# Turning the last two chunk pairs of the first token half in 64-row pieces

## The chip, the cores and the metric

The kernel runs on one core of one Trainium2 chip. The metric is device time in microseconds (us) of one execution. The engines are named as in the profile: PE (TensorE), ACT (ScalarE), DVE (VectorE), POOL (GpSimd) and SP (the engine that issues most of the loads). Each runs its own list of instructions in order, and waits on semaphores for the others.

## What is computed

One layer of a diffusion backbone: modulated RMSNorm, a mixing sub-layer (pooling and neighbourhood attention), a residual, then a squared-ReLU MLP and another residual. The change is in the MLP, at the point where its input is made:

```python
x = x + gt1 * _rmsnorm(mix_x, g_post_mix[l])
y_x = _sq_relu_mlp(_modulate(x, g_pre_mlp[l], sh2, sc2), w_mlp_in[l], w_mlp_out[l])
x = x + gt2 * _rmsnorm(y_x, g_post_mlp[l])

def _modulate(x, gain, shift, scale):
    return _rmsnorm(x, gain) * (1 + scale) + shift
def _sq_relu_mlp(h, w1, w2):
    return jnp.square(jax.nn.relu(h @ w1)) @ w2
```

There are 1024 tokens, 1024 features and 4096 hidden columns, all in float32.

## The kernel before

**Products.** Every matrix product is made of float32r pieces: an operand is split into a high part (a cast on ACT, L169 or L171) and a low part (a subtraction on DVE, L175 or L177), and `three` (L221 to L223) adds high times high, high times low and low times high. The MLP's input product is done in 2 by 2 blocks by a scheme of Strassen's kind: features in halves, tokens in halves, hidden columns in halves. B11 is the first half of the features of the first 512 tokens, B21 the second half of the features of the same tokens.

**Making B11 and B21.** The first 512 tokens lie in four pages `mp1[0..3]` of 128 tokens by 1024 features, already divided by their root mean square. The products need features on the partitions, so PE turns each 128 by 128 block against the identity. A chunk is 128 features; two chunks make a pair `kp`, four pairs in all. For one pair, `transposed` (L1647) makes eight transposes into two banks of PSUM `px`, one bank for a chunk with 512 tokens. `normal_pair` (L1656) copies each bank out on ACT with one instruction of 128 by 512, which applies the modulation as scale and shift per partition (for pairs 2 and 3 with the sign turned) into a page `nf0_<kp>`. `token_part` then casts the page (1024 wide) to its high part `thB` on ACT (L169) and subtracts for its low part `tlB` on DVE (L175). Pairs 0 and 1 make B11, pairs 2 and 3 make B21.

**The order around it.** `last_product` writes this stage by hand: the last four output products of the mixing sub-layer (`pov`, PE) stand between the transposes of pairs 0 and 1, then come pairs 2 and 3 directly behind each other. Between them stand `more()` calls, each of which splits one piece of the MLP's weights `wpA` (ACT L169 or L171, then DVE L175 or L177), and `first_less(7)` (DVE L1524), which empties the last bank `pov`. Behind `last_product` follows the first group of MLP products, two hidden blocks at a time: block 0 times B11 into bank `phx0`, block 1 times B11 into `phx1`, then block 0 times B21 added into `phx0`, block 1 times B21 into `phx1`. Twelve matmuls of 128 by 512 make one of these products. Between the first and the second product of a block, ACT copies the bank's first sum away to `s` (`first_kept`, L1893), since the scheme needs it alone; so the B21 product of a block can only begin when that copy is done.

The order on ACT and DVE is fixed to that of the program by `in_order`, and PE's as well (`first_order`). Work that is `stepwise` puts the DVE half of a split behind the next weight piece (`caught_up`), but not yet in `last_product`.

**The other half.** The second 512 tokens are turned later (`second_half`) by functions that exist already: `side_pair` (L1750) turns 64 tokens by 128 features at a time, from rows 0 to 63 of each page into one bank and from rows 64 to 127 into another, alternating between the two. `normal_sides` (L1762 on DVE, L1764 on ACT) copies out by chunk and side: four instructions of 128 by 256 for a pair, which write runs of 64 tokens. For pairs 0 and 2 one side, two of the four, goes to DVE; the rest go to ACT.

Of the kernel before, what the change touches and what calls it, by code (L numbers as in the profile page):

```python
# [13 lines left out]
AF = mybir.ActivationFunctionType  # L14
# [4 lines left out]
P = 128  # L19
# [7 lines left out]
HD = 64  # L27
# [76 lines left out]
def hybrid_block(ctx, tc, x, ctx_in, w_mod, mod_pages, w_u, b_mod, gp1, gp2, w_in, pool_w, rpb, w_out, w1, w2, vectors,  # L104
                 mask, edge, out):
    nc = tc.nc
    sub, mul, add = ALU.subtract, ALU.mult, ALU.add
# [8 lines left out]
    def cst(name, shape, dt=F32):  # L116
        return const.tile(shape, dt, tag=name, name=name)

    def sm(name, n, bufs=1):
        return small.tile([P, n], F32, tag=name.split("_")[0], name=name, bufs=bufs)  # L120

    def page(name, dt=F32):
        return act.tile([P, 1024], dt, tag="pg", name=name)
# [21 lines left out]
    ident = cst("ident", [P, P])  # L145
# [45 lines left out]
    def step_split(src, hi, lo, factor=1.0):  # L191
        high_part(src, hi, factor)
        second = lambda: low_part(src, hi, lo, factor)
        if stepwise:
            behind.append(second)
        else:
            second()
# [90 lines left out]
    def lasting(name):  # L288
        return ps_t.tile([P, 512], F32, tag="T", name=name)

    sx = cst("sx", [P, KT])
    a2, s2 = cst("a2", [P, KT]), cst("s2", [P, KT])

    with tc.tile_pool(name="ps1", bufs=6, space=PSUM) as ps1, tc.tile_pool(name="tmp1", bufs=3) as tmp:

        def bank(name):
            if name[:2] == "pm" or name in ("pxt5", "pxb2", "pxb3", "pxb4", "pxb5", "pct2", "pct3"):
                return lasting(name)
            return ps1.tile([P, 512], F32, tag="mm", name=name)
# [76 lines left out]
        on_act, on_dve = nc.scalar.copy, nc.vector.tensor_copy  # L376
# [121 lines left out]
        whole, pt = {}, {}  # L498
# [242 lines left out]
        for k in range(KT):  # L741
            for i in range(2):
                o = (k % 2) * 256 + i * P
# [423 lines left out]
    with (  # L1167
# [4 lines left out]
        bank = lasting  # L1172
# [158 lines left out]
        mp1 = {}  # L1331


        def out_sums(ps, a, w, t, begin):
            for k in range(4):
                mp = mix[a][k]
                three(ps, mp[:, t * P : (t + 1) * P], mp[:, 512 + t * P : 512 + (t + 1) * P],
                      wk(w, k, 0, 0, 512), wk(w, k, 1, 0, 512), begin and k == 0, k == 3, more=not begin)
# [32 lines left out]
        with in_order(ET.PE, ET.Activation, ET.DVE, ET.SP) as projected:  # L1371
# [31 lines left out]
            for i in range(N + 4):  # L1403
# [43 lines left out]
                else:  # L1447

                    t = i - N
# [57 lines left out]
    with tc.tile_pool(name="ps2", bufs=6, space=PSUM) as ps2:  # L1507
# [6 lines left out]
      with ExitStack() as tmp2:  # L1514
# [117 lines left out]
        less_a2, less_s2 = sm("na2", 8), sm("ns2", 8)  # L1632
# [5 lines left out]
        plain = {}  # L1638


        def transposed(kp):
            pts = []
            for o in range(2):
                k = 2 * kp + o
                pt = bank(f"px0_{k}")
                for i in range(4):
                    nc.tensor.transpose(pt[:, i * P : (i + 1) * P], mp1[i][:, k * P : (k + 1) * P], ident)  # L1647
                pts.append(pt)
            return pts

        def normal_pair(kp, pts):
            f = page(f"nf0_{kp}")
            a, d = (a2, s2) if kp < 2 else (less_a2, less_s2)
            for o, pt in enumerate(pts):
                k = 2 * kp + o
                nc.scalar.activation(f[:, o * 512 : (o + 1) * 512], pt, AF.Identity, bias=d[:, k : k + 1],  # L1656
                                     scale=a[:, k : k + 1])
            return f

        def token_part(name, kp, f):  # L1660
            hi, lo = page(f"th{name}_{kp}", F32R), page(f"tl{name}_{kp}", F32R)
            step_split(f, hi, lo)
            tok[name, kp] = hi, lo

        def pair_made(kp, pts):
            plain[0, kp] = normal_pair(kp, pts)
            token_part("B11" if kp < 2 else "B21", kp % 2, plain[0, kp])


        def first_less(t):  # L1670
            c[t, 0] = out_less(0, t, v[t - 4], u2[t - 4])

        def gate_steps(h, t):
            src = c[t] if h else c[t, 0]
            out_square(h, t, src)
            out_gated(h, t, src)

        def last_product():
            for t in range(2):
                out_sums(v[t], "A22", wt4, t, False)  # L1680
            first_less(4)
            more()
            pts = transposed(0)
            first_less(5)
            pair_made(0, pts)
            more()
            out_sums(v[2], "A22", wt4, 2, False)
            pts = transposed(1)
            first_less(6)
            gate_steps(1, 6)  # L1690
            pair_made(1, pts)
            more()
            out_sums(v[3], "A22", wt4, 3, False)
            pts = transposed(2)
            first_less(7)
            pair_made(2, pts)
            pts = transposed(3)
            more()
            pair_made(3, pts)

# [38 lines left out]
            yield  # L1739


        def side_pair(kp):
            pts = [bank(f"px1_{2 * kp + h}") for h in range(2)]
            for o in range(2):
                ks = slice((2 * kp + o) * P, (2 * kp + o + 1) * P)
                for i in range(4):
                    at = (4 * o + i) * HD
                    for h in range(2):
                        hs = slice(h * HD, (h + 1) * HD)
                        nc.tensor.transpose(pts[h][:, at : at + HD], mp1[4 + i][hs, ks], ident[hs, hs])  # L1750
            return pts

        def normal_sides(kp, pts):
            f = page(f"nf1_{kp}")
            by_side = f.rearrange("p (o i h t) -> p o h i t", o=2, i=4, h=2)
            a, d = (less_a2, less_s2) if kp < 2 else (a2, s2)
            for h in range(2):
                for o in range(2):
                    k = 2 * kp + o
                    to, pt = by_side[:, o, h], pts[h][:, o * 256 : (o + 1) * 256].rearrange("p (i t) -> p i t", i=4)  # L1760
                    if kp % 2 == 0 and h == (kp == 2):
                        nc.vector.tensor_scalar(to, pt, a[:, k : k + 1], d[:, k : k + 1], mul, add)  # L1762
                    else:
                        nc.scalar.activation(to, pt, AF.Identity, bias=d[:, k : k + 1], scale=a[:, k : k + 1])  # L1764
            return f

        def second_half():
            nf = dict((kp, normal_sides(kp, side_pair(kp))) for kp in (0, 2, 1, 3))
            return [nf[0], nf[1]], [nf[2], nf[3]]

        def second_steps(b12, b22):
            b21 = [plain[0, 2 + kp] for kp in range(2)]
            t1, t2 = [[page(f"t{i}_{kp}") for kp in range(2)] for i in (1, 2)]
            source = {"T1": t1, "T2": t2, "T3": b12, "T4": b21, "B22": b22}

            def combined(kp):
                nc.vector.tensor_tensor(t1[kp], b12[kp], plain[0, kp], add)
                add_to(b12[kp], b22[kp])
                nc.vector.tensor_tensor(t2[kp], b22[kp], t1[kp], add)
                add_to(b21[kp], t2[kp])  # L1780

            for kp in range(2):
                combined(kp)
                yield
            for name in ("T2", "T1", "T3", "B22", "T4"):
                for kp in range(2):
                    token_part(name, kp, source[name][kp])
                    yield
# [90 lines left out]
        def more():  # L1879
            ready.extend(islice(coming_parts, 1))  # L1880
# [185 lines left out]
        with tc.issue_after(added[ET.DVE]), tc.issue_after(added[ET.Activation]), in_order(ET.Activation, ET.DVE) as first_part:  # L2066
            last_product()
            stepwise.append(True)
            between, xs, ending = row_steps(), {}, None
            for p in range(0, EARLY, 2):  # L2070
                for sum in (1, 2):
                    for q in (p, p + 1):
                        if ending:
                            ending()
                        caught_up()
                        if (q, sum) == (5, 2):
                            between = second_steps(*second_half())
                        if sum == 1:
                            xs[q] = bank(f"phx{q}")
                        step(xs[q], "B11" if sum == 1 else "B21", sum == 1)  # L2080
                        next(between, None)
                        if sum == 1:
                            ending = lambda q=q: early.update({q: first_kept(q, xs[q])})
                        else:
                            ending = lambda q=q: second_kept(q, xs[q])
            ending()
            caught_up()
            for _ in between:
                caught_up()
            caught_up()  # L2090
            stepwise.clear()
# [166 lines left out]
```

## Time and profile before

| | |
|---|---|
| median of three runs | 1022.59 us (1022.5 to 1023.45) |
| the profiled execution's own time | 1022.56 us |
| its span, first to last instruction | 1020.8 us |
| around the span | 1.76 us |
| PE busy | 1010.3 us |
| ACT, DVE busy | 547.1 us, 744.4 us |
| mean granted clock of PE | 0.999 |

A row of the timeline gives the start in us from the span's start, the length in us, the engine, the line, the operation with output and input by the program's names (buffer numbers left out), and how many instructions were merged (x2). In brackets stands idle time before it and what ended it. Instructions of one engine overlap at their ends, so the distance from start to start tells what one costs in a row of them, and the length tells when its result is there.

### The profile page before, as it was taken

The page shows a single profiled execution, that of the slowest core. Times are in us where ns is not written, and L with a number is a line of the kernel's source. Part 1 is how long each engine was busy: PE and PEld are TensorE (multiplying, and loading weights), DVE is VectorE, ACT ScalarE, POOL GpSimd, SP SyncE. Part 2 cuts the span into 40 slices and gives each one's busy share as a digit, 9 for nine tenths or more (in the row PEclk, how much of TensorE's full clock was granted, in tenths as well). Part 3 has the DMA queues.
Part 4 walks back from the last instruction along what each step waited for, and adds up shares of the span by engine and source line. Part 5 has one row for each costly group of instructions (what it writes and reads, how often), then busy time and mean ns, then how long its engine had stood idle before and what let it go on. Part 6 is the DMA issues. An engine that isn't in the chain of part 4 may idle for free.

```text
span 1020.8 us, 16178 instructions
## 1 busy us (share of the span) xinstructions
PE 1010.3 (99%) x5970; PEld 834.5 (82%) x5970; DVE 744.4 (73%) x1161; ACT 547.1 (54%) x958; POOL 155.1 (15%) x235
## 2 busy tenths in 40 slices
PE   8999999999999999999999999999999999999997
PEld 5788888878998888888888888888888888888886
DVE  5588767877885688879988888755757666557576
ACT  7682255348986747786555554555543343334431
POOL 4111210166774221410000000000000000000002
PEclk9999999999999999999999999999999999999999
DMA  9899798641448945886786667437967766555555
GB/s 365 317 275 324 252 267 295 206 102 44 95 95 203 233 183 196 280 213 201 256 261 206 214 197 228 174 134 250 347 217 260 253 222 216 198 183 189 170 181 224
DMA packets 117023, 222.72 MB, mean 218 GB/s; under 512 B 9488, under 2 KB 46992, under 8 KB 116944
## 3 DMA queue, kind: packets, MB, share of 16 engines
q1 hardware_dynamic: 90448, 171.14, 49.5%
q0 software_dynamic: 9360, 19.58, 9.4%
q10 hardware_dynamic: 17136, 30.97, 8.1%
q8 instruction: 47, 0.77, 0.3%
q14 instruction: 32, 0.26, 0.1%
HBM read 168.16 MB, written 52.45 MB: 216 GB/s over the span
## 4 chain that ended last, share of the span: by engine, by line
PE 96%; DMA 2%; DVE 0%; ACT 0%; issue 0%; SPq 0%; DVEq 0%; POOLq 0%; ACTq 0%
PE pu L469 4%; PE pa L1276 4%; PE S L1196 3%; PE phx L221 3%; PE phz L221 3%; PE phv L221 3%; PE pyx L221 3%; PE phx L222 3%; PE pyz L223 3%; PE phv L222 3%; PE pyv L223 3%; PE phz L222 3%; PE pyx L223 3%; PE phx L223 3%; PE pyv L221 3%; PE pyz L221 3%
## 5 line engine op out<-in xcount | busy, mean ns | idle before, releaser
L1222 ACT ACTIVATE sp<-sp,nm 128x640 f32<-128x640 f32 (+1 forms) x64 | 51.4, 803 | 10.9 <-DVE ri L1226 5.0
L1211 DVE CUSTOM_DVE_ANT_0 sp<-S,tab 128x640 f32<-128x640 f32 (+1 forms) x56 | 44.5, 795 | 14.0 <-PE pz L1242 10.6
L169 ACT CAST wpS<-S 128x512 fp32r<-128x512 f32 x64 | 38.8, 616 | 28.2 <-PE phv L223 10.1
L1842 ACT ACTIVATE c<-c 128x512 f32<-128x512 f32 x48 | 30.3, 631 | 43.6 <-DVE c L1962 24.9
L221 PE MATMUL phx<-thB,wpA 128*128 128x512 f32 x128 | 50.3, 393 | 0.0
L222 PE MATMUL phx<-tlB,wpA 128*128 128x512 f32 x128 | 49.9, 390 | 0.0
L223 PE MATMUL phx<-thB,wpA 128*128 128x512 f32 x128 | 49.9, 390 | 0.0
L175 DVE TENSOR_TENSOR wpS<-S,wpS 128x512 fp32r<-128x512 f32 x64 | 43.4, 686 | 8.2 <-ACT wpS L169 8.2
L163 POOL TENSOR_TENSOR ry<-vy,nhalf 128x1 f32<-128x1 f32 x8 | 5.9, 740 | 281.5 <-DVE vy L161 281.5
L1843 ACT ACTIVATE c<-c 128x512 f32<-128x512 f32 x48 | 30.3, 631 | 15.2 <-DVE sa L1925 10.5
L221 PEld LDWEIGHTS phx<-thB,wpA 128*128 128x128 f32 x128 | 24.0, 188 | 5.7 <-ACT s L1893 0.6
L223 PEld LDWEIGHTS phx<-thB,wpA 128*128 128x128 f32 x128 | 24.1, 188 | 5.0
L222 PEld LDWEIGHTS phx<-tlB,wpA 128*128 128x128 f32 x128 | 24.1, 188 | 4.8
L1276 PE MATMUL pa<-pt,v 128*64 128x128 f32 x352 | 25.9, 280 | 0.2
L1261 DVE COPY pt<-T 128x512 f32<-128x512 f32 x32 | 21.9, 686 | 5.5 <-PE T L1242 5.5
L221 PE MATMUL phz<-thB,wpS 128*128 128x512 f32 x64 | 25.1, 392 | 0.0
L221 PE MATMUL phv<-thT,wpA 128*128 128x512 f32 x64 | 25.0, 391 | 0.0
L223 PE MATMUL phz<-thB,wpS 128*128 128x512 f32 x64 | 25.0, 390 | 0.0
L222 PE MATMUL phz<-tlB,wpS 128*128 128x512 f32 x64 | 24.9, 390 | 0.0
L223 PE MATMUL phv<-thT,wpA 128*128 128x512 f32 x64 | 24.9, 390 | 0.0
L222 PE MATMUL phv<-tlT,wpA 128*128 128x512 f32 x64 | 24.9, 390 | 0.0
L223 PE MATMUL phy<-thT,wpS 128*128 128x512 f32 x64 | 24.9, 390 | 0.0
(1144 smaller groups left out, 3434.3 us busy)
## 6 DMA issues: line engine op xcount, KB each, us to landing
b<-in_w SPq DMA_DIRECT2D x64, 512.0 KB, 4.1
hrS<-hdS SPq DMA_DIRECT2D x32, 512.0 KB, 5.3
hrA<-hdA SPq DMA_DIRECT2D x24, 512.0 KB, 5.3
wm<-in_mod_pages SPq DMA_DIRECT2D x16, 512.0 KB, 9.6
wa_0w<-in_w SPq DMA_DIRECT2D x16, 512.0 KB, 4.8
wa_1w<-in_w SPq DMA_DIRECT2D x16, 512.0 KB, 4.3
hdA<-c ACTq DMA_DIRECT2D x32, 256.0 KB, 2.5
hdS<-sa ACTq DMA_DIRECT2D x32, 256.0 KB, 2.5
```

Of the source, the lines that this page charges most:

```text
L169: nc.scalar.copy(hi, src)
L175: nc.vector.tensor_tensor(lo, src, hi.bitcast(F32), sub)
L221: nc.tensor.matmul(ps, ahi, bhi, start=first, stop=False, skip_group_check=more)
L222: nc.tensor.matmul(ps, ahi, blo, start=False, stop=False, skip_group_check=more)
L223: nc.tensor.matmul(ps, alo, bhi, start=False, stop=last, skip_group_check=more)
L469: nc.tensor.matmul(pus[b][j], wk(wgt, k, low, j * P, P), r, start=(k == 0 and n == 0), stop=(k == KT - 1 and n == 2))
L1196: nc.tensor.matmul(S[e][:, c0 : c0 + k[0].shape[1]], q[n_q][hs, cols], k[n_k][hs], start=(n_q + n_k == 0), stop=(n_q == 1))
L1211: nc.vector.tensor_tensor_reduce(out=to, in0=s, in1=bt, scale=1.0, scalar=BIG, op0=add, op1=ALU.min, accum_out=nm)
L1222: nc.scalar.activation(sp, sp, AF.Exp, bias=least[i, e], scale=-1.0, accum_out=sums[i][:, e : e + 1])
L1276: nc.tensor.matmul(pa[e * HD : (e + 1) * HD, cols], v[:, f : f + HD], turns[i][:, e, c] if c < 4 else fifths[i][:, :, (e + 1) * HD : (e + ...
L1842: nc.scalar.activation(r, src, AF.Relu)
L1843: nc.scalar.activation(r, r, AF.Square)
```

## The change

`side_pair` and `normal_sides` move ahead of `last_product` and take the token half `b` as an argument, with the side that DVE copies passed in. The second half calls them as before. In the first half, pairs 2 and 3 now use them: pair 2 with all four copies on ACT, pair 3 with side 1 (two copies) on DVE and side 0 on ACT. Pairs 0 and 1 keep `transposed` and `normal_pair`.

```diff
+        def side_pair(b, kp):
+            pts = [bank(f"px{b}_{2 * kp + h}") for h in range(2)]
+            for o in range(2):
+                ks = slice((2 * kp + o) * P, (2 * kp + o + 1) * P)
+                for i in range(4):
+                    at = (4 * o + i) * HD
+                    for h in range(2):
+                        hs = slice(h * HD, (h + 1) * HD)
+                        nc.tensor.transpose(pts[h][:, at : at + HD], mp1[4 * b + i][hs, ks], ident[hs, hs])
+            return pts
+
+        def normal_sides(b, kp, pts, on_dve):
+            f = page(f"nf{b}_{kp}")
+            by_side = f.rearrange("p (o i h t) -> p o h i t", o=2, i=4, h=2)
+            a, d = (less_a2, less_s2) if (kp < 2) == (b == 1) else (a2, s2)
+            for h in range(2):
+                for o in range(2):
...
+                    if h == on_dve:
+                        nc.vector.tensor_scalar(to, pt, a[:, k : k + 1], d[:, k : k + 1], mul, add)
+                    else:
+                        nc.scalar.activation(to, pt, AF.Identity, bias=d[:, k : k + 1], scale=a[:, k : k + 1])
+            return f
+
         def pair_made(kp, pts):
-            plain[0, kp] = normal_pair(kp, pts)
+            plain[0, kp] = normal_pair(kp, pts) if kp < 2 else normal_sides(0, kp, pts, (None, 1)[kp - 2])
             token_part("B11" if kp < 2 else "B21", kp % 2, plain[0, kp])
...
-            pts = transposed(2)
+            pts = side_pair(0, 2)
             first_less(7)
             pair_made(2, pts)
-            pts = transposed(3)
+            pts = side_pair(0, 3)
             more()
             pair_made(3, pts)
...
         def second_half():
-            nf = dict((kp, normal_sides(kp, side_pair(kp))) for kp in (0, 2, 1, 3))
+            nf = dict((kp, normal_sides(1, kp, side_pair(1, kp), (0, None, 1, None)[kp])) for kp in (0, 2, 1, 3))
```

On PE, behind the last `pov` product, pair 2 stood before as eight transposes of whole blocks, one bank after the other (`px_4` and `px_5` are the banks, `mp_0` to `mp_3` the pages of tokens; a row's size is that of its output):

```order
L1647 MATMUL px_4_5239<-ident,mp_0_4632 128x128
L1647 MATMUL px_4_5239<-ident,mp_1_4642 128x128
L1647 MATMUL px_4_5239<-ident,mp_2_4652 128x128
L1647 MATMUL px_4_5239<-ident,mp_3_4656 128x128
L1647 MATMUL px_5_5244<-ident,mp_0_4632 128x128
L1647 MATMUL px_5_5244<-ident,mp_1_4642 128x128
L1647 MATMUL px_5_5244<-ident,mp_2_4652 128x128
L1647 MATMUL px_5_5244<-ident,mp_3_4656 128x128
```

Now it begins with these eight, and the same eight follow for the second chunk; pair 3 goes in the same way into `px_6` and `px_7`:

```order
L1668 MATMUL px_4_5239<-ident,mp_0_4632 128x64
L1668 MATMUL px_5_5240<-ident,mp_0_4632 128x64
L1668 MATMUL px_4_5239<-ident,mp_1_4642 128x64
L1668 MATMUL px_5_5240<-ident,mp_1_4642 128x64
L1668 MATMUL px_4_5239<-ident,mp_2_4652 128x64
L1668 MATMUL px_5_5240<-ident,mp_2_4652 128x64
L1668 MATMUL px_4_5239<-ident,mp_3_4656 128x64
L1668 MATMUL px_5_5240<-ident,mp_3_4656 128x64
```

So 16 transposes become 32, and both banks of a pair are finished only with the pair's last two transposes, where the first bank was finished after four of eight.

On ACT, from the weight piece ahead of pair 2 to the copy that frees `phx0` for its B21 product, stood before:

```order
L171 ACTIVATE wpA_0_5224<-wa0w 128x512
L1656 ACTIVATE nf_2_5251<-px_4_5239,ns_5067,na_5066 128x512
L1656 ACTIVATE nf_2_5251<-px_5_5244,ns_5067,na_5066 128x512
L169 CAST thB_0_5254<-nf_2_5251 128x1024
L171 ACTIVATE wpA_1_5268<-wa1w 128x512
L1656 ACTIVATE nf_3_5271<-px_6_5258,ns_5067,na_5066 128x512
L1656 ACTIVATE nf_3_5271<-px_7_5263,ns_5067,na_5066 128x512
L169 CAST thB_1_5274<-nf_3_5271 128x1024
L169 CAST wpA_2_5281<-wa2w 128x512
L1893 COPY s_0_5295<-phx_5278 128x512
```

and now stands:

```order
L171 ACTIVATE wpA_0_5224<-wa0w 128x512
L1682 ACTIVATE nf_2_5259<-px_4_5239,ns_5067,na_5066 128x4x64 x2
L1682 ACTIVATE nf_2_5259<-px_5_5240,ns_5067,na_5066 128x4x64 x2
L169 CAST thB_0_5264<-nf_2_5259 128x1024
L171 ACTIVATE wpA_1_5286<-wa1w 128x512
L1682 ACTIVATE nf_3_5289<-px_6_5268,ns_5067,na_5066 128x4x64 x2
L169 CAST thB_1_5294<-nf_3_5289 128x1024
L169 CAST wpA_2_5301<-wa2w 128x512
L1893 COPY s_0_5315<-phx_5298 128x512
```

Two copies of pair 2 became four, each half as wide; two copies of pair 3 became two, each half as wide. Nothing else on ACT moved. The cast `thB_1` reads the whole page `nf_3`, which DVE now writes in part.

On DVE, in the same stretch (`co_7` is `first_less(7)`), stood before:

```order
L1524 TENSOR_TENSOR co_7_5249<-pov_4913,so_1_4390 128x512
L175 TENSOR_TENSOR tlB_0_5255<-nf_2_5251,thB_0_5254 128x1024
L177 SCALAR_TENSOR_TENSOR wpA_1_5268<-wa1w,wpA_1_5268 128x512
L175 TENSOR_TENSOR tlB_1_5275<-nf_3_5271,thB_1_5274 128x1024
L175 TENSOR_TENSOR wpA_2_5281<-wa2w,wpA_2_5281 128x512
```

and now stands:

```order
L1524 TENSOR_TENSOR co_7_5257<-pov_4913,so_1_4390 128x512
L175 TENSOR_TENSOR tlB_0_5265<-nf_2_5259,thB_0_5264 128x1024
L177 SCALAR_TENSOR_TENSOR wpA_1_5286<-wa1w,wpA_1_5286 128x512
L1680 TENSOR_SCALAR nf_3_5289<-px_7_5269,na_5066,ns_5067 128x4x64 x2
L175 TENSOR_TENSOR tlB_1_5295<-nf_3_5289,thB_1_5294 128x1024
L175 TENSOR_TENSOR wpA_2_5301<-wa2w,wpA_2_5301 128x512
```

DVE's two copies of pair 3 stand behind the low part of pair 2 (`tlB_0`) and a weight piece (`wpA_1`). In the rest of the program the engines' rows are the same as before, in the same order.

More of the change, by code (lines that the diff above doesn't have):

```diff
@@ L1658, in normal_pair @@
             return f
+        def side_pair(b, kp):
[14 more added lines that the diff above has]
+                for o in range(2):
+                    k = 2 * kp + o
+                    to, pt = by_side[:, o, h], pts[h][:, o * 256 : (o + 1) * 256].rearrange("p (i t) -> p i t", i=4)
+                    if h == on_dve:
[3 more added lines that the diff above has]
+            return f
         def token_part(name, kp, f):
@@ L1739, in row_steps @@
             yield
[L1742 to L1765, printed above, removed]
         def second_half():
-            nf = dict((kp, normal_sides(kp, side_pair(kp))) for kp in (0, 2, 1, 3))
+            nf = dict((kp, normal_sides(1, kp, side_pair(1, kp), (0, None, 1, None)[kp])) for kp in (0, 2, 1, 3))
             return [nf[0], nf[1]], [nf[2], nf[3]]
```

## The prediction

> **What bounds the kernel now.** I read the page first, for the engine that carries the span.
>
> ```profile
> span 1020.8 us, 16178 instructions
> PE 1010.3 (99%) x5970; PEld 834.5 (82%) x5970; DVE 744.4 (73%) x1161; ACT 547.1 (54%) x958; POOL 155.1 (15%) x235
> PE 96%; DMA 2%; DVE 0%; ACT 0%; issue 0%; SPq 0%; DVEq 0%; POOLq 0%; ACTq 0%
> ```
>
> PE carries the chain that ended last. By these shares, time saved on PE is gained and time added on ACT or DVE is free. But shares are averages, so I looked at the stage itself: the waits of PE from the changed place to the end, and the busy times of the stage from the first changed transpose to the end of the first four B products.
>
> ```profile
> PE px L1750 <- PE px L1750: 0.2, 1, 0.2
> ```
>
> ```profile
> 398.66:411.44 12.78, 12.78 (x66) 10.64 (x65) 9.60 (x15) 11.09 (x21) 0.86 (x1) 1.00 0.41 125
> ```
>
> PE is said to wait for 0.2 us in 622 us. In the stage ACT (the fourth busy time) works 11.09 of 12.78 us. An engine so full, with a fixed order, can be the one for which PE waits next. So I read the timeline of each engine there. PE:
>
> ```profile
> 398.43 0.40 PE L223 MATMUL pov<-to_1h,A 128*128 128x512 f32 x1
> 398.66 1.91 PE L1647 MATMUL px<-ident,mp 128*128 128x128 f32 x16
> 400.33 0.47 PE L221 MATMUL phx<-thB,wpA 128*128 128x512 f32 x1
> ...
> 405.65 0.39 PE L223 MATMUL phx<-thB,wpA 128*128 128x512 f32 x1
> 405.88 0.46 PE L221 MATMUL phx<-thB,wpA 128*128 128x512 f32 x1
> 406.17 0.40 PE L222 MATMUL phx<-tlB,wpA 128*128 128x512 f32 x1
> ```
>
> The sixteen transposes take 1.67 us from the first to the product behind them (398.66 to 400.33). The matmul at 405.88 opens the B21 product of block 0, and its successor comes 0.29 us later where 0.23 is the rule (405.65 to 405.88): this matmul was held for 0.06 us. What held it shows on ACT:
>
> ```profile
> 398.12 0.63 ACT L171 ACTIVATE wpA<-wa0w 128x512 fp32r<-128x512 f32 x1
> 399.30 1.45 ACT L1656 ACTIVATE nf<-px,ns,na 128x512 f32<-128x512 f32 x2 [0.55 <-PE px L1647]
> 400.78 1.05 ACT L169 CAST thB<-nf 128x1024 fp32r<-128x1024 f32 x1
> 401.73 0.63 ACT L171 ACTIVATE wpA<-wa1w 128x512 fp32r<-128x512 f32 x1
> 402.26 1.43 ACT L1656 ACTIVATE nf<-px,ns,na 128x512 f32<-128x512 f32 x2
> 403.73 1.05 ACT L169 CAST thB<-nf 128x1024 fp32r<-128x1024 f32 x1
> 404.68 0.62 ACT L169 CAST wpA<-wa2w 128x512 fp32r<-128x512 f32 x1
> 405.20 0.58 ACT L1893 COPY s<-phx 128x512 f32<-128x512 f32 x1
> ```
>
> From 399.30 to 405.78 ACT has no gap, and its last row here is the copy that must have read `phx0` before the B21 product may add to it. It ends at 405.78, and PE goes on 0.10 us later at the earliest. **So PE and ACT arrive at this point together**: what makes ACT later here makes PE later, one for one; what makes PE earlier makes it wait. The change touches both, and DVE:
>
> ```profile
> 399.39 0.68 DVE L177 SCALAR_TENSOR_TENSOR wpA<-wa0w,wpA 128x512 fp32r<-128x512 f32 x1
> 399.99 0.68 DVE L1524 TENSOR_TENSOR co<-pov,so 128x512 f32<-128x512 f32 x1
> 401.86 1.23 DVE L175 TENSOR_TENSOR tlB<-nf,thB 128x1024 fp32r<-128x1024 f32 x1 [1.18 <-ACT thB L169]
> 403.00 0.68 DVE L177 SCALAR_TENSOR_TENSOR wpA<-wa1w,wpA 128x512 fp32r<-128x512 f32 x1
> 404.81 1.23 DVE L175 TENSOR_TENSOR tlB<-nf,thB 128x1024 fp32r<-128x1024 f32 x1 [1.13 <-ACT thB L169]
> ```
>
> DVE has over 1 us idle ahead of each low part, but in a fixed order: the low part of pair 2 must be done before DVE comes to what stands behind it.
>
> **What the new pieces cost.** The trace has them already, in the second token half: 64-row transposes (48 and 16 in a row), half-wide copies on ACT (four and four) and on DVE (two).
>
> ```profile
> 430.25 0.39 PE L223 MATMUL phx<-thB,wpA 128*128 128x512 f32 x1
> 430.57 1.71 PE L1750 MATMUL px<-ident,mp 64*128 64x64 f32 x48
> 432.46 0.71 PE L1750 MATMUL px<-ident,mp 64*128 64x64 f32 x16 [0.18 <-PE px L1750]
> 433.10 0.50 PE L221 MATMUL phx<-thB,wpA 128*128 128x512 f32 x1
> ```
>
> ```profile
> 431.31 0.99 DVE L1762 TENSOR_SCALAR nf<-px,na,ns 128x256 f32<-128x256 f32 x2 [1.01 <-PE px L1750]
> ```
>
> ```profile
> 434.20 1.94 ACT L1764 ACTIVATE nf<-px,ns,na 128x256 f32<-128x256 f32 x4
> 436.00 1.97 ACT L1764 ACTIVATE nf<-px,s,a 128x256 f32<-128x256 f32 x4
> ```
>
> **PE.** The lead-in of the 64-row transposes is 0.32 us (430.25 to 430.57) against 0.23 for a normal step, so 0.09 more. Sixteen take 1.71 / 48 x 16 = 0.57 us, and sixteen with the hand-over to the next product 0.64 (432.46 to 433.10). Together 0.09 + 0.57 + 0.64 = 1.30 us for 32, against 1.67: **PE gains 0.37 us** up to the B11 products. It would reach the B21 product at 405.51 if nothing held it there.
>
> [...]
>
> **ACT, pair 2.** The first copy needs both sides of the pair turned. In the second half DVE began its first copy 1.06 us after the last normal matmul began (430.25 to 431.31), so here at 398.43 + 1.06 = 399.49, which is 0.19 later than 399.30. Four half-wide copies take 1.94 us and the cast follows 0.03 behind (as 399.30 + 1.45 = 400.75 was followed at 400.78): cast at 399.49 + 1.97 = 401.46, which is 0.68 late. Of this 0.49 (1.97 less 1.48) is the price of four copies for two: their start-to-start is 1.80 / 4 = 0.45 us, not half of a wide one's.
>
> **ACT and DVE, pair 3.** ACT's two copies would start at 402.26 + 0.68 = 402.94 and end at 403.98 (the second starts 0.45 later and lasts 0.59, which is 1.94 less three times 0.45). With that the lateness would fall to 0.28. But the cast of pair 3 now also needs DVE's two copies. DVE takes up the low part of pair 2 at 401.46 + 1.05 + 0.03 = 402.54 (0.03 as at 401.86, behind the cast's end at 401.83), the weight piece 1.14 later at 403.68 (401.86 to 403.00), and its first copy 0.60 later at 404.28 (399.39 to 399.99). Two copies last 0.99, so to 405.27; with 0.03 again for the hand-over ACT casts at **405.30 instead of 403.73: 1.57 us late**. ACT idles from 403.98 on.
>
> **The end of the stage.** Behind the cast nothing on ACT changes (wpA cast, copy of `phx0`), so the copy ends at 407.35 and the B21 product begins its work 1.57 us later than before. PE, which could have been there at 405.51, waits some 2 us; its gain of 0.37 lies inside the wait. The low part of pair 3 also moves by 1.57 together with the cast, and it was needed only half a product behind the point at which PE waits, so it stays as far ahead of PE as it was. The same holds for the next hand-over (`phx1`): ACT's, DVE's and PE's rows are all shifted by the same amount.
>
> **The sum.** 0.19 (later first copy) + 0.49 (four copies for two) + 0.89 (pair 3's cast waits for DVE; with two wide copies as before it would stand at 404.41) = 1.57 us, made against the profiled execution's own 1022.56 (span 1020.8): 1024.13. The median shown is 1022.59, so 1024.2 us, or 0.15% more. **The bounds**: if each half-wide copy costs just half of a wide one, 0.49 falls away (1.08); if it costs its whole length unoverlapped, it is at most 0.63 instead of 0.45, so 0.7 more (2.3):
>
> ```profile
> L1764 ACT ACTIVATE nf<-px,s,a x6: 562/606/626, 433.3 to 437.3; 128x256 f32<-128x256 f32 x6
> ```
>
> That makes 1023.7 to 1024.9. A difference of 0.2%, 2.05 us, is about what a measurement of this kernel can tell from no change, and this forecast lies inside it.
>
> **Rivals.**
>
> *Given back later.* If PE met other waits downstream that do not move, the delay would shrink. The only ones between 406 and the end are small: steps of 0.34 to 0.38 us instead of 0.23.
>
> ```profile
> 452.43 0.51 PE L221 MATMUL phx<-thB,wpA 128*128 128x512 f32 x1
> 452.77 0.40 PE L222 MATMUL phx<-tlB,wpA 128*128 128x512 f32 x1
> ...
> 466.37 0.50 PE L221 MATMUL phz<-thB,wpS 128*128 128x512 f32 x1
> ```
>
> There are three such places, near 452, 466 and 469, each 0.11 us at the step shown and some 0.15 just ahead of it, 0.8 in all at most: +0.8, 1023.4 us. They hang on ACT and DVE, which are late too, so it is unlikely.
>
> *PE's gain alone shows.* If ACT were not what holds the B21 product, the time would be 1022.59 - 0.37 = 1022.2. The 0.06 us of hold at 405.88 and the copy's end at 405.78 speak against it.
>
> *The copies of pair 3 really run side by side*: if DVE were free at 402.94, ACT would cast at 404.01, only 0.28 late: 1022.9. It decides whether DVE's two copies stand ahead of pair 2's low part, and in the order they stand behind it. [...]
>
> *Slower, by the clock.* If PE's idle 2 us made its clock fall, the product behind it would run at half speed: twelve steps of 0.23 more, 2.7 us, so 1.57 + 2.7 = +4.3, 1026.9 us. It decides from the idle time at which the clock falls. The trace speaks against: the first 5 us hold 1.57 us of idle PE at a granted clock of 1.00.
>
> ```profile
> 0.00:5.00 5.00, 3.43 (x4) 1.51 (x5) 0.23 (x3) 1.34 (x2) 0.95 (x7) 1.00 0.61 188
> ```
>
> [...]
>
> **Chances.** Forecast 0.75 (one in six of it above 1024.64), given back later 0.10, PE's gain alone 0.03, side by side 0.04, clock 0.04, another slow-down behind the stage 0.03, something faster 0.01. Slower by over 0.2%: 0.12 + 0.04 + 0.03 = 0.19; faster by over 0.2%: 0.01; within 0.2%: 0.80. The range takes in the forecast with its bounds and the delay partly given back, with some 0.2 to 0.4 us for the scatter of the runs (1022.5 to 1023.45): 1022.9 to 1025.1.
>
> **What would show it.** Right: ACT idle ahead of the second `thB` cast (L169), ended by DVE's copies (L1680), with the cast near 405.3; PE idle some 2 us ahead of the first B21 matmul, the largest wait behind 398 us, ended by ACT's copy L1893; the 32 transposes done in about 1.3 us; all that follows later by the same 1.5 us or so. Wrong: a PE that runs on at 405.5 without a gap, DVE copies ahead of 404, half-wide copies on ACT far from 0.45 us apart, a granted clock below 1.00 behind the gap, or a gap that closes again by 470.

## The result and the profile after

The changed kernel takes 1024.65 us (median of 13 runs, 1023.85 to 1026.66), the kernel before 1022.54 us (13 runs, 1022.31 to 1023.45). The ratio is 1.0024 with a 95% interval of 1.0016 to 1.0032: slower by 1.6 to 3.3 us. The forecast was 1024.2 us, the range 1022.9 to 1025.1.

The 13 runs fall into two groups, and a second series of the same kernel does so again (11 runs beside 15 of the kernel before on the same chip: ratio 1.0021, 1.0012 to 1.0030). Of the 24, 13 lie between 1023.85 and 1024.65 (median 1024.36) and 11 between 1025.48 and 1026.66 (median 1025.96), with nothing between. The lower group has the forecast's time. The upper group has a second cost of 1.6 us, and its mean granted clock (the share of full speed that PE was given) is lower: 0.996 to 0.998 in its runs, 0.998 or 0.999 in the others'. The prediction had such a cost as a rival with a chance of 0.04. The profiled execution, 1025.48 us, belongs to the upper group, so its profile shows both.

The first part of the page, and the waits of PE from the changed place to the end:

```profile
span 1023.7 us, 16211 instructions
PE 1010.1 (99%) x5986; PEld 833.8 (81%) x5986; DVE 745.0 (73%) x1163; ACT 547.4 (53%) x960; POOL 155.0 (15%) x235
```

```profile
PE phx L221 <- ACT s L1893: 1.8, 1, 1.8
PE px L1668 <- PE px L1668: 0.2, 1, 0.2
```

The shares have not moved, and they couldn't show this: one wait of 1.8 us, at the first B21 product, for ACT's copy of `phx0`. The timeline of PE around it:

```profile
398.14 0.39 PE L223 MATMUL pov<-to_1h,A 128*128 128x512 f32 x1
398.46 1.21 PE L1668 MATMUL px<-ident,mp 64*128 64x64 f32 x32
399.60 0.50 PE L221 MATMUL phx<-thB,wpA 128*128 128x512 f32 x1
...
404.99 0.39 PE L223 MATMUL phx<-thB,wpA 128*128 128x512 f32 x1
407.17 0.56 PE L221 MATMUL phx<-thB,wpA 128*128 128x512 f32 x1 [1.79 <-ACT s L1893]
407.53 0.63 PE L222 MATMUL phx<-tlB,wpA 128*128 128x512 f32 x1
407.96 0.63 PE L223 MATMUL phx<-thB,wpA 128*128 128x512 f32 x1
...
410.92 0.39 PE L221 MATMUL phx<-thB,wpA 128*128 128x512 f32 x1
411.15 0.40 PE L222 MATMUL phx<-tlB,wpA 128*128 128x512 f32 x1
...
433.16 0.39 PE L223 MATMUL phx<-thB,wpA 128*128 128x512 f32 x1
```

Two things stand here. The wait ends at 407.17. And behind it the matmuls lie 0.43 us apart (407.53 to 407.96) instead of 0.23, until 410.92. That is a clock at about half its rate, and the windows say so. The columns are the stretch, its length, then busy us and instructions of PE, PEld, DVE, ACT and POOL, then PE's granted clock, the DMA share and GB/s:

```profile
404.06:407.47 3.41, 1.62 (x7) 1.05 (x6) 2.25 (x5) 2.05 (x3) 0.00 (x0) 1.00 0.52 152
407.47:410.88 3.41, 3.41 (x9) 2.64 (x8) 2.98 (x6) 2.96 (x8) 0.86 (x1) 0.50 0.29 103
410.88:414.29 3.41, 3.41 (x16) 2.80 (x15) 2.54 (x4) 1.73 (x4) 0.00 (x0) 1.00 0.48 150
```

The clock is 1.00, then 0.50 for 3.41 us, then 1.00. It falls at 407.47, when PE has been back at work for 0.3 us.

**A measure for the stage.** Single executions differ ahead of this stage: the last `pov` matmul starts between 397.77 and 398.94 in the profiles. So all profiles are compared by the distance from the last `pov` matmul to the last matmul ahead of the second half's turn. Before it was 31.82 us (the rows at 398.43 and 430.25 in the prediction), now it is 433.16 - 398.14 = 35.02, so +3.20. Of this the slow stretch has 1.55: the eight steps from 407.53 to 410.92 take 3.39 us, where eight of 0.23 take 1.84. That leaves +1.65 without it. From there to the end of the span lie 590.55 us before (1020.8 - 430.25) and 590.54 after: nothing is gained or given back behind the stage.

The chain that ACT and DVE form, as the prediction drew it:

```profile
399.21 1.93 ACT L1682 ACTIVATE nf<-px,ns,na 128x256 f32<-128x256 f32 x4 [0.75 <-PE px L1668]
401.18 1.05 ACT L169 CAST thB<-nf 128x1024 fp32r<-128x1024 f32 x1
402.13 0.63 ACT L171 ACTIVATE wpA<-wa1w 128x512 fp32r<-128x512 f32 x1
402.66 1.00 ACT L1682 ACTIVATE nf<-px,ns,na 128x256 f32<-128x256 f32 x2
405.07 1.05 ACT L169 CAST thB<-nf 128x1024 fp32r<-128x1024 f32 x1 [1.41 <-issue]
...
406.54 0.58 ACT L1893 COPY s<-phx 128x512 f32<-128x512 f32 x1
```

```profile
402.25 1.23 DVE L175 TENSOR_TENSOR tlB<-nf,thB 128x1024 fp32r<-128x1024 f32 x1 [1.87 <-ACT thB L169]
403.40 0.69 DVE L177 SCALAR_TENSOR_TENSOR wpA<-wa1w,wpA 128x512 fp32r<-128x512 f32 x1
404.00 0.99 DVE L1680 TENSOR_SCALAR nf<-px,na,ns 128x256 f32<-128x256 f32 x2
```

ACT is done with its half of pair 3 at 403.66 and casts at 405.07, 0.08 us behind the end of DVE's copies at 404.99. The profile puts that idle time down to "issue"; the order of DVE's rows and the ends of the two show what it was.

### The profile page after: what moved, and what is told of

Its sections match the earlier page's. It is cut to its first block, busy times and chain, and to the rows that moved or that the text cites. A ratio compares the mean times of both kernels' runs of the same rounds, so it can differ in the third digit from the quotient of the medians.

```text
span 1023.7 us, 16211 instructions
## 1 busy us (share of the span) xinstructions
PE 1010.1 (99%) x5986; PEld 833.8 (81%) x5986; DVE 745.0 (73%) x1163; ACT 547.4 (53%) x960; POOL 155.0 (15%) x235
## 4 chain that ended last, share of the span: by engine, by line
PE 96%; ACT 1%; DVE 1%; DMA 1%; issue 1%; POOL 0%; SPq 0%; DVEq 0%; POOLq 0%; ACTq 0%
PE pu L469 4%; PE pa L1276 4%; PE S L1196 3%; PE phz L221 3%; PE phv L221 3%; PE pyx L221 3%; PE pyx L223 3%; PE pyv L222 3%; PE pyz L222 3%; PE phz L223 3%; PE pyx L222 3%; PE phv L223 3%; PE pyv L223 3%; PE pyz L223 3%; PE pyz L221 3%; PE pyv L221 3%
## 5 line engine op out<-in xcount | busy, mean ns | idle before, releaser
L221 PE MATMUL phx<-thB,wpA 128*128 128x512 f32 x128 | 50.8, 397 | 1.8 <-ACT s L1893 1.8
L223 PE MATMUL phx<-thB,wpA 128*128 128x512 f32 x128 | 50.5, 394 | 0.0
L221 PEld LDWEIGHTS phx<-thB,wpA 128*128 128x128 f32 x128 | 24.4, 191 | 7.8 <-ACT s L1893 2.6
L223 PEld LDWEIGHTS phx<-thB,wpA 128*128 128x128 f32 x128 | 24.5, 191 | 5.2
L221 PE MATMUL phz<-thB,wpS 128*128 128x512 f32 x64 | 25.0, 391 | 0.0
L221 PE MATMUL phv<-thT,wpA 128*128 128x512 f32 x64 | 25.0, 391 | 0.0
L223 PE MATMUL phz<-thB,wpS 128*128 128x512 f32 x64 | 24.9, 389 | 0.0
L221 PE MATMUL phy<-thT,wpS 128*128 128x512 f32 x64 | 24.9, 389 | 0.0
L222 PE MATMUL phy<-tlT,wpS 128*128 128x512 f32 x64 | 24.9, 389 | 0.0
```

The lines of the kernel that those rows point to most:

```text
L221: nc.tensor.matmul(ps, ahi, bhi, start=first, stop=False, skip_group_check=more)
L222: nc.tensor.matmul(ps, ahi, blo, start=False, stop=False, skip_group_check=more)
L223: nc.tensor.matmul(ps, alo, bhi, start=False, stop=last, skip_group_check=more)
```

## The experiments

Two theories were to be tested. **Queue**: PE waits because ACT's cast of pair 3 waits for DVE's copies, which stand behind pair 2's low part, and each us of lateness on ACT is one on PE. **Clock by idle PE**: the wait itself brings the clock down in about half of the executions. Rivals: the 64-row form costs the time wherever the copies are made, and the clock falls because of the 64-row transposes or by chance. None of the edits leaves out work.

### DVE out of pair 3

```diff
-            plain[0, kp] = normal_pair(kp, pts) if kp < 2 else normal_sides(0, kp, pts, (None, 1)[kp - 2])
+            plain[0, kp] = normal_pair(kp, pts) if kp < 2 else normal_sides(0, kp, pts, None)
```

> Pair 3's four copies all on ACT, DVE out of it; the 64-row transposes and the half-wide copies stay. Theory (queue): PE waits because pair 3's cast on ACT waits for DVE's copies, which stand behind the low part of pair 2. Then the cast comes at 402.66 + 1.97 = 404.63 on the changed kernel's scale instead of 405.07, PE's wait shrinks by 0.44 from 1.79 to some 1.35 us, and the time at full clock is about 1.2 over the kernel before, 1023.7. Theory (clock by idle PE): the granted clock still falls in some executions, in fewer than in the changed kernel's (6 of 13). Rival (form): the half-wide, 64-row form itself costs the time wherever the copies are made; then the wait stays at 1.8 us or grows, 1024.3 or more at full clock.

Measured: 1023.53 us (11 runs, 1023.16 to 1025.37), ratio 1.0014 (1.0005 to 1.0023). Stage +1.16. The wait of PE, and ACT's copies of pair 3 with the cast behind them:

```profile
PE phx L221 <- ACT s L1893: 1.4, 1, 1.4
```

```profile
402.28 1.91 ACT L1682 ACTIVATE nf<-px,ns,na 128x256 f32<-128x256 f32 x4
404.23 1.05 ACT L169 CAST thB<-nf 128x1024 fp32r<-128x1024 f32 x1
```

The cast comes 404.23 - 397.77 (this profile's last `pov` matmul) = 6.46 us behind that matmul, against 6.93 in the changed kernel: giving the work to DVE made it later, as expected to 0.03 us. Eight runs lie at 1023.16 to 1023.94; three lie at 1024.45, 1025.0 and 1025.37. Whether those had a slow stretch can't be told: their mean clocks (0.998, 0.999, 0.998) are no lower than the others', and of the 33 runs of the kernel before beside them two also stood at 1024.35 and 1024.36. What made them longer stays open.

### DVE's copies of pair 3 ahead of pair 2's low part

```diff
             first_less(7)
-            pair_made(2, pts)
+            plain[0, 2] = normal_sides(0, 2, pts, None)
             pts = side_pair(0, 3)
+            plain[0, 3] = normal_sides(0, 3, pts, 1, None, (1,))
+            token_part("B21", 0, plain[0, 2])
             more()
-            pair_made(3, pts)
+            normal_sides(0, 3, pts, 1, plain[0, 3], (0,))
+            token_part("B21", 1, plain[0, 3])
```

`normal_sides` gets the page and the sides to copy as two more arguments, so that DVE's side can be written ahead of ACT's.

> As the changed kernel, but DVE's two copies of pair 3 stand ahead of pair 2's low part. Theory (queue): ACT casts pair 3 right behind its own two copies, at 402.66 + 1.07 = 403.73 instead of 405.07; PE's wait shrinks from 1.79 to some 0.45 us; the time is 0.2 to 0.4 over the kernel before, 1022.8. Theory (clock by idle PE): no execution shows a lower clock, since the wait is short. Rival (form): still 1 us or more over the kernel before. Rival (clock by the 64-row transposes): about half of the executions still lose some 1.5 us to a lower clock.

Measured: 1022.83 us (11 runs, 1022.40 to 1023.49), ratio 1.0002 (0.9994 to 1.0011). Stage +0.27. PE's wait, and ACT's rows:

```profile
PE phx L221 <- ACT s L1896: 0.4, 1, 0.4
```

```profile
402.94 1.00 ACT L1682 ACTIVATE nf<-px,ns,na 128x256 f32<-128x256 f32 x2
403.98 1.05 ACT L169 CAST thB<-nf 128x1024 fp32r<-128x1024 f32 x1
```

The same instructions in another order on DVE, and ACT casts 0.04 us behind its own copies. The stage falls from +3.20, or +1.65 without the clock, to +0.27, and no run lies over 1023.5. This shows the queue: of the 1.65 us, 1.38 hung on two DVE instructions being behind two others. The rival "form" is out as the cause of that; with all copies on ACT, in the run before this one, the same form still cost 1.16.

### PE kept busy through the wait

```diff
+                        if (q, sum) == (0, 2):
+                            warm, hi = bank("warm"), tok["B11", 0][0]
+                            for _ in range(8):
+                                nc.tensor.matmul(warm, hi[:, 512:640], hi[:, :512], start=True, stop=True)
                         step(xs[q], "B11" if sum == 1 else "B21", sum == 1)
```

> As the changed kernel, with eight more matmuls of 128x512 (1.8 us) into a bank of their own, in PE's order just ahead of the first B21 product, where it waits for 1.79 us; their result is not read. Theory (clock by idle PE): PE is busy through the wait, the granted clock is 1.00 throughout, and every execution lies at 1.6 to 1.9 over the kernel before, 1024.2 to 1024.5, with no group at 1025.5 and above. Rival (clock by the 64-row transposes, or by chance): about half of the executions still show a lower clock and 1025.5 or more. If the wait were shorter than 1.8 us, the time would grow by the rest.

Measured: 1024.05 us (11 runs, 1023.67 to 1024.35), ratio 1.0015 (1.0006 to 1.0024), so 1.55 over the kernel before beside it, a little under the 1.6 to 1.9 expected. Stage +1.63. PE, and its windows:

```profile
405.05 1.98 PE L2083 MATMUL warm<-thB 128*128 128x512 f32 x8
407.01 0.50 PE L221 MATMUL phx<-thB,wpA 128*128 128x512 f32 x1
407.34 0.40 PE L222 MATMUL phx<-tlB,wpA 128*128 128x512 f32 x1
```

```profile
405.00:409.00 4.00, 4.00 (x18) 2.97 (x18) 3.02 (x5) 3.60 (x7) 0.00 (x0) 1.00 0.63 197
```

Eight useless matmuls in the gap, and the upper group is gone: none of 11 runs over 1024.4, where 11 of 24 were without them. With the same transposes ahead of it, the clock stays at 1.00 in this profile, in which PE does not idle. What is left, 1.63 us, is the wait alone.

### ACT made late in the kernel before

```diff
             more()
-            pair_made(3, pts)
+            plain[0, 3] = normal_pair(3, pts)
+            late = out_junk(0, 8)
+            for _ in range(2):
+                nc.scalar.copy(late, pts[1])
+            token_part("B21", 1, plain[0, 3])
```

This is the kernel before with two, three, four or five copies on ACT, so that PE waits at the same place without any 64-row transposes ahead of it.

> The kernel before, with two more copies of a bank on ACT (128x512, their result is not read) ahead of the cast of pair 3; no 64-row transposes and no work of DVE added in the first half. They make ACT some 1.2 us late (0.58 each and the hand-over), so PE waits for some 1.2 us at the first B21 product. Theory (one for one): the time is 1.2 over the kernel before, 1023.7. Theory (clock by idle PE, judged in fixed stretches of some 3.3 us, as long as the slow stretch of the changed kernel, and falling where over half of a stretch is idle): no execution has the lower clock. Rival (any idle of over 1 us can bring the clock down): some executions lie 1.5 us higher.

> The same with three copies: ACT some 1.8 us late and PE waiting as long as in the changed kernel, but without its 64-row transposes. Theory (clock by idle PE): as in the changed kernel, about half of the executions at 1024.3 and the others at 1025.5 to 1026.5. Rival (the clock falls because of the 64-row transposes ahead of the wait): all executions near 1024.3 at full clock.

> The kernel before with four more copies on ACT ahead of the cast of pair 3 (the runs with three and five gave waits of PE of 1.38 and 2.61 us, so this one waits for some 2.0), without 64-row transposes. Theory (stretches): the clock is judged in fixed stretches of 3.42 us, as long as the slow stretch in both profiles that have one, and falls for the next stretch where more than half, 1.71 us, was idle. A wait of 2.0 us leaves that much in one stretch with a chance of 2.0 / 3.42 = 0.58: some 6 of 11 executions at 1022.5 + 2.1 + 1.5 = 1026.1, the others at 1024.7. Rival (64-row transposes help the fall): none or one of 11, all near 1024.7. Rival (the length alone decides, from some point between 1.4 and 2.6 us): all or none.

> The same with five copies: ACT some 3.05 us late, PE waits for 3 us. Theory (clock by idle PE in fixed stretches): most executions, some 8 in 10, have the lower clock for one stretch, so the median is 1022.5 + 3.05 + 1.5 = 1027, a few at 1025.6. Rival (64-row transposes needed): 1025.6 in all. Rival (the wait is given back later): under 1025.

| extra copies | PE's wait, us | stage in the profile | runs, us | ratio (95%) |
|---|---|---|---|---|
| 2 | 0.76 | +1.00 | 11: 1022.87 to 1023.93, median 1023.44 | 1.0010 (1.0001 to 1.0019) |
| 3 | 1.38 | +1.57 | 11: 1023.96 to 1024.52, median 1024.28 | 1.0016 (1.0007 to 1.0025) |
| 4 | 1.99 | +3.78 | 5: 1025.39, 1025.66, 1026.22, 1026.49, 1026.89 | 1.0032 (1.0020 to 1.0045) |
| 5 | 2.61 | +4.27 | 5: 1025.37, 1026.52, 1027.21, 1027.44, 1027.53 | 1.0042 (1.0029 to 1.0054) |

I had taken a copy's lateness for PE's wait. In the listing of waits 0.2 us of it is not counted, since the matmul before has its own length to run out (0.39 us, at steps of 0.23): three copies make ACT 1.6 us late, but the wait is 1.38. So the run with three was not the equal of the changed kernel that it was meant to be, and its 11 runs without an upper group say nothing of the transposes. The run with four closes that: with 1.99 us of wait and no 64-row transposes ahead of it, three of five runs have a mean clock of 0.996 to 0.998 and lie 0.6 to 1.5 us above the other two, and its profile has the same stretch of 3.41 us at 0.50 as that with five:

```profile
404.63:408.04 3.41, 1.42 (x7) 0.89 (x6) 1.19 (x2) 3.13 (x6) 0.00 (x0) 1.00 0.56 153
408.04:411.45 3.41, 3.41 (x9) 2.63 (x10) 3.11 (x7) 2.83 (x7) 0.75 (x1) 0.50 0.21 81
```

```profile
404.51:407.92 3.41, 1.05 (x5) 0.55 (x3) 0.77 (x1) 3.35 (x6) 0.00 (x0) 1.00 0.50 145
407.92:411.33 3.41, 3.16 (x8) 2.49 (x9) 3.41 (x7) 2.61 (x8) 0.33 (x1) 0.50 0.20 77
```

The 64-row transposes are not needed for the clock to come down: it does so here without them. With five runs each, the counts for four and five copies are rough, and the two shorter runs with four copies lie 0.7 to 1.0 us over the 1024.7 expected at full clock, which stays open.

### The changed kernel again

No edit.

> The changed kernel itself once more, to count. Theory (stretches): its wait of 1.79 us lies within one stretch of 3.42 us with a chance of (3.42 - 1.79) / 3.42 = 0.48, by the rule of over half idle 0.52; so some 5 or 6 of 11 executions near 1025.7 and the others near 1024.2, with nothing between beyond the scatter of 0.4 us. Rival (an accident of the first chip): all near 1024.2.

Measured: 1024.60 us (11 runs); six at 1023.88 to 1024.60, five at 1025.96 to 1026.42. The profiled one is of the five, and shows best when the clock falls:

```profile
405.32 0.39 PE L223 MATMUL phx<-thB,wpA 128*128 128x512 f32 x1
407.55 0.50 PE L221 MATMUL phx<-thB,wpA 128*128 128x512 f32 x1 [1.84 <-ACT s L1893]
407.88 0.39 PE L222 MATMUL phx<-tlB,wpA 128*128 128x512 f32 x1
...
408.81 0.51 PE L223 MATMUL phx<-thB,wpA 128*128 128x512 f32 x1
409.12 0.63 PE L221 MATMUL phx<-thB,wpA 128*128 128x512 f32 x1
409.55 0.63 PE L222 MATMUL phx<-tlB,wpA 128*128 128x512 f32 x1
```

```profile
405.56:408.97 3.41, 1.57 (x7) 1.21 (x7) 2.44 (x4) 3.01 (x6) 0.00 (x0) 0.99 0.71 223
408.97:412.38 3.41, 3.41 (x10) 2.62 (x9) 2.56 (x5) 2.96 (x9) 0.86 (x1) 0.50 0.24 89
```

PE works at full clock again from 407.55, for 1.4 us, and only then the clock falls, at 408.93 (the first window ends just behind that, so it reads 0.99). Behind the first profile's wait, as long within 0.05 us, it fell 0.30 us after PE's return (407.17 to 407.47); with four copies 0.17 us after it (407.87 to 408.04), with five 0.25 us ahead of it (407.92, the return at 408.17). In the order of the waits (1.79, 1.84, 1.99 and 2.61 us) the 3.41 us ahead of the fall hold 1.62, 1.57, 1.42 and 1.05 us of work. Any 3.41 us that hold the whole wait of 1.38 us with three copies have 3.41 - 1.38 = 2.03 us of work, and any others more; there the clock stays at 1.00:

```profile
404.00:408.00 4.00, 2.62 (x12) 1.88 (x11) 1.77 (x3) 3.54 (x7) 0.00 (x0) 1.00 0.45 131
408.00:412.00 4.00, 4.00 (x19) 3.22 (x19) 3.23 (x7) 3.60 (x11) 0.86 (x1) 1.00 0.36 135
```

With pair 3 all on ACT (a wait of 1.4 us) the matmuls of these products are as long in the mean as with three copies (393, 389 and 389 ns on L221 to L223), where this profile with a fall has 398, 394 and 394. No execution of the lower group was profiled.

The clock also falls at the end of the span, where PE has no more work. In the profile of the changed kernel in the section on the result, PE's last matmul ends at 1017.40, and the fall comes 4.46 us later:

```profile
1017.41:1021.86 4.45, 0.00 (x0) 0.00 (x0) 2.17 (x4) 0.69 (x2) 0.55 (x1) 1.00 0.28 103
1021.86:1023.70 1.84, 0.00 (x0) 0.00 (x0) 0.00 (x0) 0.00 (x0) 0.00 (x0) 0.50 0.10 36
```

In the kernel before it comes 3.29 us after the last matmul (1014.50 to 1017.79). The expectations take the clock to be judged in fixed stretches and to fall where over half of one was idle, and get chances of 0.52 for the wait of 1.79 us and 0.58 for 2.0 from that. The counts agree (11 of 24 and 3 of 5), and so do falls at different distances from PE's return; but the fixed stretches and the half are the author's estimate, and no run shows either by itself.

### Both pairs shared, DVE ahead

```diff
+            stepwise.append(True)
             more()
+            stepwise.clear()
             out_sums(v[3], "A22", wt4, 3, False)
             pts = side_pair(0, 2)
-            first_less(7)
-            pair_made(2, pts)
+            plain[0, 2] = normal_sides(0, 2, pts, 1)
+            caught_up()
             pts = side_pair(0, 3)
+            plain[0, 3] = normal_sides(0, 3, pts, 1, None, (1,))
+            token_part("B21", 0, plain[0, 2])
+            first_less(7)
             more()
-            pair_made(3, pts)
+            normal_sides(0, 3, pts, 1, plain[0, 3], (0,))
+            token_part("B21", 1, plain[0, 3])
```

The first of two runs has this without the three lines of `stepwise` and `caught_up`, which put one low part of weights behind DVE's copies of pair 2.

> The 64-row form with side 1 of both pairs copied on DVE, ahead of the low part of pair 2 and ahead of the emptying of the last bank pov (L1524). Theory (queue): ACT has two copies for each pair; DVE is free at 399.71 and done with pair 2 at 400.7, the cast of pair 3 comes at about 403.2 on the changed kernel's scale (403.44 would be the kernel before's), PE reaches the B21 product 0.37 us earlier and is held for 0.1 us or so; the time is 0.2 to 0.35 under the kernel before, 1022.2 to 1022.35, at full clock. Rival (form): same as before or slower.

> As the version with side 1 of both pairs on DVE ahead of the low parts (measured at 0.08 under the kernel before), with one more move: the low part of the weight piece wpA of block 0 (L177, 0.6 us) goes behind DVE's copies of pair 2, so that these begin when ACT's do. Theory (queue): the cast of pair 2 no longer waits 0.56 us for DVE, ACT's copy of phx0 ends ahead of PE's arrival, and PE keeps its whole gain of 0.37 us: 1022.1 to 1022.2. Rival (PE's gain is worth nothing here): 1022.4 or more.

Measured: the first 1022.42 us (11 runs, 1022.02 to 1023.89), ratio 1.0000 (0.9991 to 1.0009), stage -0.17; that is 0.08 us under the kernel before where 0.2 to 0.35 was expected, since ACT waited 0.56 us for DVE ahead of pair 2's cast. The second 1022.13 us (11 runs, 1021.53 to 1023.01), ratio 0.9994 (0.9985 to 1.0003), stage -0.49. Its ACT rows:

```profile
400.01 1.02 ACT L1682 ACTIVATE nf<-px,ns,na 128x256 f32<-128x256 f32 x2 [0.75 <-PE px L1668]
401.13 1.05 ACT L169 CAST thB<-nf 128x1024 fp32r<-128x1024 f32 x1
...
402.62 1.00 ACT L1682 ACTIVATE nf<-px,ns,na 128x256 f32<-128x256 f32 x2
403.65 1.06 ACT L169 CAST thB<-nf 128x1024 fp32r<-128x1024 f32 x1
```

Both casts follow ACT's own copies at once, and PE keeps what the 64-row transposes save. By the stage of its profile and by the median (0.44 under the kernel before's) it is the fastest of all, but its interval holds 1, so it is not shown to be faster.

## Why the prediction was right, and where not

- **PE's gain, 0.37 us forecast.** From the last `pov` matmul to the first product: 399.60 - 398.14 = 1.46 us against 400.33 - 398.43 = 1.90, so 0.44. It lies inside the wait, as said; the last version shows that it is real.
- **First copy 0.19 later.** 399.21 - 398.14 = 1.07 against 0.87: 0.20. **Four copies for two, 0.49.** The cast follows the first copy by 1.97 us, as computed.
- **Pair 3's cast waits for DVE, 0.89.** Measured 0.08 us for the hand-over from DVE to ACT where 0.03 was taken from the other direction; the rest fits. In all the cast is 1.63 us late (6.93 behind the last `pov` matmul against 5.30), for 1.57.
- **One for one on PE, nothing given back.** Stage +1.63 in the version without idle PE; behind the stage 590.5 us in both.
- **The sum.** 13 of 24 runs have a median of 1024.36, for the forecast 1024.2. The mechanism and its size were right for them. That the median of all runs lies in the range too was luck: in both series it is the slowest run of the lower group, the seventh of 13 (1024.65) and the sixth of 11 (1024.60). With one of those runs in the upper group it would lie at 1025.4 or more, above the range.
- **The step that failed** is the clock rival's: "The trace speaks against: the first 5 us hold 1.57 us of idle PE at a granted clock of 1.00", with a chance of 0.04 and a price of 2.7 us. That row was misread: by the length of its weight loads PE did not run at full clock there. In the slow stretch of the changed kernel (407.47 to 410.88), PE's weight loads (PEld) take 0.33 us, and 0.19 around it. In the kernel before, those of the first matmuls take 0.34 us and stand 0.85 us apart up to the last one at 6.85:

```profile
4.29 0.34 PEld L365 LDWEIGHTS pm<-ones,ident 128*128 128x128 f32 x1 [0.52 <-issue]
5.15 0.34 PEld L365 LDWEIGHTS pm<-ones,ident 128*128 128x128 f32 x1 [0.52 <-issue]
```

In the changed kernel's profile the same loads change to 0.19 us, 0.43 us apart, from 4.93 on:

```profile
4.29 0.34 PEld L365 LDWEIGHTS pm<-ones,ident 128*128 128x128 f32 x1 [0.52 <-issue]
4.93 0.19 PEld L365 LDWEIGHTS pm<-ones,ident 128*128 128x128 f32 x1 [0.30 <-issue]
```

So the 1.00 of the view does not hold for the first 5 us, and says nothing against a fall. The trace of the kernel before also has a fall: the clock is 0.50 from 1017.79 on, 3.29 us after PE's last matmul ends at 1014.50. And 1.57 us of idle is less than the shortest wait behind which a profile shows a fall, 1.79 us, while the forecast had some 2 us for the wait: the row could say nothing of a wait that long. The prediction lists "a granted clock below 1.00 behind the gap" among the signs of being wrong, and the profiled execution shows it.
- **The price of a fall** was forecast at 2.7 us, twelve slow steps. The slow stretch ends after 3.41 us, within the product, and costs 1.55 us in the profile and 1.60 between the medians of the groups. Since nearly half of the runs pay it, the median moves from +1.8 to +2.1 us, and over the 0.2% (2.05 us) inside which the forecast lay; the interval of the ratio holds both sides of that.

## What to carry to other kernels

Where an engine's list is fixed, work handed to a less busy engine arrives when its place in that list comes up, not when the engine is idle: place it ahead of whatever waits for another engine. Here the cast of pair 3 stood 6.93 us behind the last `pov` matmul with DVE's copies behind the low part of pair 2, and 5.55 us (403.98 - 398.43) with them ahead of it. Look for the point at which two engines arrive together; there the later one sets the time, and a saving on the other is worth nothing until it is moved too: PE's 0.44 us lay inside the wait of the changed kernel, and the stage became shorter than before, by 0.17 and 0.49 us, only where ACT's casts came earlier too. The wait of PE of 1.8 us cost another 1.6 us through the clock in 11 of 24 executions (in the profiles with waits of 1.4 and 1.38 us the clock did not fall); eight useless matmuls in the gap removed that part in all of 11 runs, and run times that fall into two groups were the sign of it.

## What the runs showed of the chip

- In the four profiles in which PE waited 1.79 us or more in the midst of work, the granted clock fell to 0.50 for one stretch of 3.41 us. In the changed kernel it fell 0.30 us (407.17 to 407.47) and 1.38 us (407.55 to 408.93) after PE had taken up work again. Behind the last matmul of the span it fell after 4.46 us in the changed kernel and 3.29 us in the kernel before.
- How many executions lay in an upper group, by the length of PE's wait in the profile: 1.38 us none of 11, 1.8 us 11 of 24, 1.99 us 3 of 5, 2.61 us 4 of 5; at 1.4 us three of 11 are undecided. With eight matmuls in the wait it was none of 11. No run tried a wait between 1.4 and 1.79 us.
- The view gave a granted clock of 1.00 for the first 5 us of the kernel before, while weight loads took 0.34 us there instead of 0.19.
- A half-wide copy on ACT (128x256 out of PSUM, runs of 64 written) costs 0.45 us from start to start, a wide one (128x512) 0.68 (1.45 for two, of which one lasts 0.77): two halves cost 0.22 us more than a whole.
